# Splitting the query and key fetches of a hybrid decoder trunk, with full-height score products and new planner costs

## The chip, the cores and the metric

The kernel runs on one core of one Trainium2 chip. The metric is the device time of one execution in microseconds (us); several executions are timed and their median is given. TensorE (PE) multiplies, VectorE (DVE), ScalarE (ACT) and GpSimd (POOL) work elementwise, and DMA transfers are issued from the queues of SyncE (SP), POOL and ACT.

## The reference

The reference is a decoder trunk of two layers on 512 tokens of 1024 channels. Each layer is FFN, token mixer, FFN, each followed by a layer norm. The mixer has three head groups that read one projection and feed one output projection:

```python
x = layer_norm(ALPHA * x + 0.5 * swiglu(x, gate_a, up_a, down_a))
aq, ak, av, bq, bk, bv, cc = split(x @ w_in)
o_a = diff_attention(rope(aq), rope(ak), av, lam)    # 6 heads, two softmax maps each, q and k 32 wide
o_b = dilated_attention(rope(bq), rope(bk), bv)      # 6 heads, q and k 64 wide, three dilation patterns
o_c = rwkv7_mixer(cc, ...)                           # 4 heads, recurrent state 64 x 64 per head
x = layer_norm(ALPHA * x + concat(o_a, o_b, o_c) @ w_out)
x = layer_norm(ALPHA * x + 0.5 * swiglu(x, gate_b, up_b, down_b))
```

## The kernel before, in words

All big products are float32 made of three products of rounded parts: a value is split into a high part (rounded to the fast float32r form) and a low part (the rest), and hi x hi, hi x lo and lo x hi are added up (`mm3`). The FFNs are written as plain loops. They take most of the time and the change leaves them alone.

The mixer of each layer is different. It is written as some 24 Python generators (`columns` for the input projection, `turner`, `fetch`, `attend` for both attention groups, `keys`, `inside`, `invert`, `scan`, `rwkv_out` for the recurrent group, `out` for the output projection, and more). `Board.merge` runs them against a table of estimated costs and estimated free times. It always takes the first generator in a fixed rank that is ready by these estimates, and so fixes the order in which every engine gets its instructions. On the chip each engine then works strictly in that written order, and waits where an operand is not there yet. An estimate that is wrong therefore costs nothing by itself; it only changes the order.

Queries and keys of the two attention groups go a detour. `turner` transposes them on PE, splits them into a high and a low part in a tile `z`, and SP stores them to memory (`qkA`, `qkB`, three head pairs each). `fetch`, on POOL's queue, loads them back, one head (`e` is 0 or 1 in the pair `hp`) at a time, in the arrangement that the score product needs. A fetch waits for the pair's stores and for two free slots of the tag `x` (four in all). On POOL the fetches stand in one line with the computation of the low parts of the weights (`wl`) and with the masks of the recurrent group (`x<-am`).

For group A the contraction is 96 rows high: rows 0 to 31 hold hi, 32 to 63 lo, 64 to 95 hi of the query, against hi, hi and lo of the key. Before, two transfers per tile fill this, and the first has a source whose outermost dimension counts 2 (stride `256 * S` between the high and low parts for the query, stride 0 for the key, so that it is read twice):

```python
dma(a[0:64], ap(d, hi, [[256 * S, 2], [2 * S, 32], [1, 2 * S]]))
dma(b[0:64], ap(d, hi + k, [[0, 2], [2 * S, 32], [1, 2 * S]]))
```

For group B the query's hi and lo stand above each other in 128 rows and meet the key's hi in both halves; a second product of 64 rows adds the query's hi times the key's lo (`b`, 64 rows).

Each POOL transfer signals on one of eight semaphores, taken in turn; a transfer waits until the one eight places before it has landed.

`scan` walks the recurrent group's eight chunks of 64 tokens: each needs the state of the one before, and `sgm` is that state times the decay. `rwkv_out` normalizes each pair of chunks (tiles `gy`, `yc`), and `mixer_tiles_c` transposes `yc` on PE (`m<-kept,yc`) for the output projection. The second half of the scan loads its tiles `kr` back from memory through SP's queue.

Of the kernel before, what the change touches and what calls it, by code (L numbers as in the profile page):

```python
# [369 lines left out]
class Board:  # L370
# [36 lines left out]
    def note(self, name, fn, aps, cost):  # L407
        at = self.free[name]
        tiles = [self.ready.setdefault(a.tensor.name, [0.0, "", 0.0, None]) for a in aps]
        assert all(r[3] != "dropped" for r in tiles)  # L410
        dma = fn == "dma_start"
        for r in tiles[dma and tiles[0][1] == "dma":]:
            if r[1] != name or name != "pe":
                at = max(at, r[0] + 0.134)
        end = at + cost
        self.free[name] = end
        if dma:
            n = 4
            for d in aps[0].shape:
                n *= d  # L420
            end = max(end, self.free["dma"]) + n / 340e3
            self.free["dma"] = end
            end += 2.0
        for r in tiles:
            r[2] = max(r[2], end)
        tiles[0][0] = max(tiles[0][0], end)
        tiles[0][1] = "dma" if dma else name
        if dma:
            self.late = max(self.late, end)
        elif name != "pe":  # L430
            self.last = max(self.last, end)
# [45 lines left out]
class Watched:  # L477
# [5 lines left out]
    def __getattr__(self, fn):  # L483
        call = getattr(self.engine, fn)

        def run(*args, **kw):
            aps = [a for a in list(args) + list(kw.values()) if hasattr(a, "tensor") and hasattr(a, "shape")]
            n = 1
            for a in aps:
                m = 1  # L490
                for d in a.shape[1:]:
                    m *= d
                n = max(n, m)
            if self.name == "pe":
                n = 1
                for d in aps[0].shape[1:]:
                    n *= d
                rate = 2 if fn == "transpose" else 1 if aps[2].dtype == FR and n >= 256 else 4
                cost = rate * n / 2400.0 + (0.009 if rate == 4 else 0.003)
            elif fn == "dma_start":  # L500
                cost = {"pool": 1.04, "act": 0.5, "sp": 0.47}[self.name]
            elif fn == "reciprocal":
                cost = 0.06 + n / 160.0
            else:
                cost = {"vec": 0.07 + n / 960.0, "act": 0.12 + n / 1400.0, "pool": 0.1 + n / 720.0}[self.name]
                if fn == "activation" and "accum_out" in kw:
                    cost += 0.1
                if fn == "tensor_tensor" and self.name == "pool":
                    cost = 0.1 + n / 450.0
            self.board.note(self.name, fn, aps, cost)  # L510
            return call(*args, **kw)  # L511

        return run
# [7 lines left out]
class Mix:  # L521
# [247 lines left out]
    def fetch(self):  # L769

        dma = self.gps.dma_start
        ap = lambda t, off, dims: bass.AP(tensor=t.tensor, offset=t.offset + off, ap=dims)
        for grp in "AB":
            for hp in range(3):
                for e in range(2):
                    yield f"qk{grp}{hp}", "x", "x"
                    if (hp, e) == (0, 0):
                        yield f"qk{grp}{hp}", "x", "x", "bias"
                        self.bias = self.get("bias", "bias")
                        dma(self.bias, self.tr.consts[:, 130:642] if grp == "A" else self.tr.consts[:, 642:1154])  # L780
                    a = self.get("x", "q", (128, 2, S))
                    d = self.qk[grp, hp]
                    hi, lo, k = e * 64 * S, (256 + e * 64) * S, 128 * S
                    if grp == "A":
                        b = self.get("x", "k", (128, 2, S))
                        dma(a[0:64], ap(d, hi, [[256 * S, 2], [2 * S, 32], [1, 2 * S]]))
                        dma(b[0:64], ap(d, hi + k, [[0, 2], [2 * S, 32], [1, 2 * S]]))
                        dma(a[64:96], ap(d, hi, [[2 * S, 32], [1, 2 * S]]))
                        dma(b[64:96], ap(d, lo + k, [[2 * S, 32], [1, 2 * S]]))
                    else:  # L790
                        b = self.get("x", "k2", (64, S))
                        dma(a[:, 0, :], ap(d, hi, [[256 * S, 2], [S, 64], [1, S]]))
                        dma(a[:, 1, :], ap(d, hi + k, [[0, 2], [S, 64], [1, S]]))
                        dma(b, ap(d, lo + k, [[S, 64], [1, S]]))
                    self.qkt[grp, hp, e] = a.bitcast(FR), b.bitcast(FR)
                    self.mark(f"q{grp}{hp}{e}")

# [308 lines left out]
    def scan(self):  # L1106

        vec, act, pe, sp = self.vec, self.act, self.pe, self.sp
        u, drop, kr, am, bt, yt, gam = self.u, self.drop, self.kr, self.am, self.bt, self.yt, self.gam
        st = None  # L1110
        yield "yt0"
        for ch in range(8):
            hf, cc = divmod(ch, 4)
            if cc == 0:
                yield "u", "u"
                for j in range(2):
                    kr[j, hf] = u("kr", (128, 4, 2, 64))
                    sp.dma_start(kr[j, hf].rearrange("p c e t -> p (c e t)"), self.kd[j, hf])
                yield f"yt{hf}", kr[0, hf], kr[1, hf]
            yield f"uv{ch // 2}"  # L1120
            uv, vt = self.uv[ch // 2]
            uvc = uv[:, ch % 2]
            heads = [(h, h // 2, HALF[h % 2], HALF[1 - h % 2], am[hf, h % 2, cc // 2][:, cc % 2, h // 2]) for h in range(4)]
            yield ".", "r"
            z = self.acc("r", (128, 2, 64))
            for h, j, s, f, a_ in heads:
                pe.matmul(z[f, j, :], a_[s, 0:64], uvc[s, h, :], start=True, stop=st is None)
                if st is not None:
                    pe.matmul(z[f, j, :], kr[j, hf][s, cc, 0, :], st[s, j, :], start=False, stop=True)
            zs = self.t("zs", (128, 2, 64), bufs=2)  # L1130
            act.copy(zs, z)
            drop(z)
            yield ".", "r"
            ups = self.acc("r", (128, 2, 64))
            for h, j, s, f, a_ in heads:
                pe.matmul(ups[f, j, :], yt[hf][f, cc * 2 + j, :], zs[f, j, :], start=True, stop=True)
            act.mul(uvc[HALF[1], 0::2], ups[HALF[1]], -1.0)
            vec.tensor_scalar(uvc[HALF[0], 1::2], ups[HALF[0]], -1.0, None, op0=OP.mult)
            drop(ups)
            nst = None  # L1140
            if ch < 7:
                yield ".", "r", "st"
                ps = self.acc("r", (128, 2, 64))
                for h, j, s, f, a_ in heads:
                    pe.matmul(ps[s, j, :], bt[hf, cc // 2][:, cc % 2, j, s], uvc[:, h, :], start=True, stop=True)
                nst = self.get("st", "st", (128, 2, 64))
                for j in range(2):
                    gj = gam[j][:, ch:ch + 1]
                    if st is None:
                        vec.tensor_scalar(nst[:, j, :], ps[:, j, :], gj, None, op0=OP.mult)  # L1150
                    else:
                        vec.scalar_tensor_tensor(nst[:, j, :], ps[:, j, :], gj, sgm[:, j, :], op0=OP.mult, op1=OP.add)
                drop(ps)
                if ch < 6:
                    sgm = self.t("sgm", (128, 2, 64), bufs=2)
                    for j in range(2):
                        vec.tensor_scalar(sgm[:, j, :], nst[:, j, :], gam[j][:, ch + 1:ch + 2], None, op0=OP.mult)
            if cc == 3:
                drop(yt[hf], bt[hf, 0], bt[hf, 1])
            self.chunks.append((ch, uv, st, heads, kr, vt, am))  # L1160
            self.mark(f"chunk{ch}")
            st = nst
# [62 lines left out]
    def attend(self, grp):  # L1225
# [6 lines left out]
        def scores(x):  # L1232
# [7 lines left out]
            for m in range(M):  # L1240
                sc = self.acc("p1")
                if isA:
                    pe.matmul(sc[:, :nn], a[0:96, m, qs], b[0:96, m, :nn], start=True, stop=True)
                else:
                    pe.matmul(sc[:, :nn], a[:, 0, qs], a[:, 1, :nn], start=True, stop=False)
                    pe.matmul(sc[:, :nn], a[0:64, 0, qs], b[:, :nn], start=False, stop=True)
                t = self.get("t", "t")
                nm = self.t("nm", (128, 1), bufs=8)
                vec.tensor_tensor_reduce(t[:, :n], sc[:, :n], bias[:, S - n:], scale, 3e38, op0=OP.add, op1=OP.min,
# [300 lines left out]
```

## Time and profile before

| what | value |
|---|---|
| median of 3 runs | 2329.84 us (2324.28 to 2331.13) |
| the profiled execution's own time | 2319.83 us |
| its span, first to last instruction | 2318.0 us |
| PE busy | 2215.6 us (96% of the span) |
| mean granted clock of PE | 0.975 |
| DVE, ACT, POOL busy | 49%, 35%, 14% |
| mixer of layer 0 and of layer 1 | about 376 to 800 us and 1523 to 1957 us |

The profiled execution is 10.0 us faster than the median of the timed runs. Times in rows are microseconds from the start of the span. A busy PE is a PE with a product in its pipeline, which says nothing of the clock that it has: a granted clock of 1.00 is 2.4 GHz, 0.50 is 1.2 GHz.

### The profile page before, as it was taken

Reading aid. Unit: us, or ns where it says so; the run is one execution under the profiler, and the core shown is the slowest. Engines: PE = TensorE matmul, PEld = TensorE weight load, DVE = VectorE, ACT = ScalarE, POOL = GpSimd, SP = SyncE. Lnnn points to the kernel's source line nnn. Section 1 sums busy time; section 2 is a strip of 40 time slices with the busy share of each in tenths; the row PEclk is TensorE's granted clock in tenths of the full one; section 3 lists DMA queues with packets and bytes.
Section 4 is the critical chain, followed back from the end, with each engine's and each line's share of the span. In section 5 each row is a group of like instructions: output and inputs, shape, how many; then the busy total and the mean of one; then the engine's idle time right before and its main releaser. Section 6 shows DMA issues by size and latency. Waiting matters only on the chain.

```text
span 2318.0 us, 31736 instructions
## 1 busy us (share of the span) xinstructions
PE 2215.6 (96%) x12384; PEld 1863.6 (80%) x12384; DVE 1146.8 (49%) x2483; ACT 803.4 (35%) x1559; POOL 317.5 (14%) x344
## 2 busy tenths in 40 slices
PE   9999999988899999999999999999878999999998
PEld 8888888787776788888888888887877867888886
DVE  3333346766566633333653332656765666333336
ACT  4322223435444323222433222343444443222222
POOL 1000002343232200000010000033432322000000
PEclk9999999999899999999999999999987999999999
DMA  5333344354433323332543333432553323233334
GB/s 171 101 102 98 113 137 146 102 136 98 104 106 101 118 74 94 98 99 91 173 120 108 101 96 109 155 128 85 136 108 94 107 95 119 84 98 91 100 109 154
DMA packets 253030, 258.34 MB, mean 111 GB/s; under 512 B 45562, under 2 KB 202304, under 8 KB 252880
## 3 DMA queue, kind: packets, MB, share of 16 engines
q1 hardware_dynamic: 221488, 228.20, 32.4%
q0 software_dynamic: 30816, 27.06, 4.8%
q8 instruction: 97, 1.59, 0.3%
q10 hardware_dynamic: 576, 1.05, 0.1%
q14 instruction: 53, 0.43, 0.1%
HBM read 233.85 MB, written 22.28 MB: 110 GB/s over the span
## 4 chain that ended last, share of the span: by engine, by line
PE 80%; DVE 8%; DMA 5%; issue 4%; POOL 1%; ACT 1%; SPq 0%; POOLq 0%; DVEq 0%; ACTq 0%
PE p L87 18%; PE p L86 18%; PE p L85 18%; PE p L511 13%; PE m L511 4%; PE r L511 3%; DMA k<-qkA 3%; PE r L86 2%; PE r L85 2%; PE r L87 2%; DMA k<-qkB 1%; DVE x L511 1%; POOL wl L511 1%; DMA q<-qkB 0%; DVE x L146 0%
## 5 line engine op out<-in xcount | busy, mean ns | idle before, releaser
L80 DVE TENSOR_TENSOR lo<-raw,hi 128x1024 fp32r<-128x1024 f32 x300 | 366.2, 1223 | 627.8 <-ACT hi L79 627.5
L87 PE MATMUL p<-xhi,lo 128*128 128x512 f32 (+1 forms) x1392 | 535.7, 385 | 0.0
L86 PE MATMUL p<-xlo,hi 128*128 128x512 f32 (+1 forms) x1392 | 533.7, 383 | 0.7 <-DVE xlo L126 0.7
L85 PE MATMUL p<-xhi,hi 128*128 128x512 f32 (+1 forms) x1392 | 533.6, 383 | 0.5 <-ACT xhi L125 0.5
L79 ACT CAST hi<-raw 128x1024 fp32r<-128x1024 f32 x300 | 315.6, 1053 | 583.5 <-PE p L86 258.1
L86 PEld LDWEIGHTS p<-xlo,hi 128*128 128x128 f32 x1392 | 261.7, 188 | 56.3 <-DVE xlo L126 1.1
L85 PEld LDWEIGHTS p<-xhi,hi 128*128 128x128 f32 x1392 | 261.8, 188 | 53.8 <-ACT xhi L125 1.0
L87 PEld LDWEIGHTS p<-xhi,lo 128*128 128x128 f32 x1392 | 261.9, 188 | 52.6
L511 POOL TENSOR_TENSOR wl<-wr,wh 128x512 fp32r<-128x512 f32 x152 | 203.8, 1360 | 670.1 <-ACT wh L511 629.3
L511 PE MATMUL p<-wh,xhi 128*128 128x256 f32 (+1 forms) x704 | 233.7, 332 | 1.4 <-DVE rb L511 1.1
L511 PE MATMUL p<-wh,xlo 128*128 128x256 f32 (+1 forms) x704 | 218.9, 311 | 0.5 <-DVE xlo L511 0.4
L511 PE MATMUL p<-wl,xhi 128*128 128x256 f32 (+1 forms) x704 | 218.5, 310 | 0.0
L87 PE MATMUL p<-hi,hl 128*128 128x512 f32 x528 | 205.8, 390 | 0.0
L86 PE MATMUL p<-lo,hh 128*128 128x512 f32 x528 | 205.8, 390 | 0.0
L85 PE MATMUL p<-hi,hh 128*128 128x512 f32 x528 | 205.7, 390 | 0.0
L511 PEld LDWEIGHTS p<-wh,xhi 128*128 128x128 f32 x704 | 138.9, 197 | 12.7 <-PE p L511 1.5
L511 PEld LDWEIGHTS p<-wh,xlo 128*128 128x128 f32 x704 | 138.7, 197 | 7.6 <-DVE xlo L511 2.2
L246 DVE TENSOR_TENSOR hr<-p,hr 128x512 f32<-128x512 f32 x88 | 60.8, 691 | 167.3 <-PE p L87 156.9
L511 PEld LDWEIGHTS p<-wl,xhi 128*128 128x128 f32 x704 | 139.2, 198 | 4.3
L247 ACT CAST hh<-hr 128x512 fp32r<-128x512 f32 x88 | 54.3, 617 | 205.9 <-DVE hr L246 195.8
L511 ACT ACTIVATE t<-t,nm 128x128 f32<-128x128 f32 (+3 forms) x144 | 80.2, 557 | 125.0 <-DVE nm L511 124.0
L85 PEld LDWEIGHTS p<-hi,hh 128*128 128x128 f32 x528 | 99.1, 188 | 20.6
(253 smaller groups left out, 3061.0 us busy)
## 6 DMA issues: line engine op xcount, KB each, us to landing
raw<-in_ffn_a_down SPq DMA_DIRECT2D x66, 512.0 KB, 3.3
raw<-in_ffn_b_down SPq DMA_DIRECT2D x66, 512.0 KB, 3.3
raw<-in_ffn_a_gate SPq DMA_DIRECT2D x44, 512.0 KB, 3.8
raw<-in_ffn_a_up SPq DMA_DIRECT2D x44, 512.0 KB, 3.9
raw<-in_ffn_b_gate SPq DMA_DIRECT2D x40, 512.0 KB, 3.9
raw<-in_ffn_b_up SPq DMA_DIRECT2D x40, 512.0 KB, 3.8
wr<-in_w_in SPq DMA_DIRECT2D x56, 256.0 KB, 3.1
wr<-in_w_in SPq DMA_DIRECT2D x24, 512.0 KB, 3.8
```

Of the source, the lines that this page charges most:

```text
L79: nc.scalar.copy(hi, raw)
L80: (vec or nc.vector).tensor_tensor(lo, raw, hi.bitcast(FT), op=OP.subtract)
L85: mm(out, lh, rh, start=first, stop=False)
L86: mm(out, lh, rl, start=False, stop=False)
L87: mm(out, ll, rh, start=False, stop=last)
L246: nc.vector.tensor_tensor(hr, acc[1, f], hr, op=OP.mult)
L247: nc.scalar.copy(hi, hr)
L511: return call(*args, **kw)
```

## The change

The fetches of group A become six transfers of 32 rows per head instead of four, those of group B six of 64 rows instead of three; no source has an outermost dimension of 2 any more. Group B's low key stands in both halves of a tile of 128 rows, so that the second score product has 128 rows too (it adds lo x lo, which was left out before). The decayed state `sgm` is computed by ACT instead of DVE. And the planner's costs of PE products, POOL transfers and the transfer rate are changed, which orders the mixer of both layers anew.

```diff
-            end = max(end, self.free["dma"]) + n / 340e3
+            end = max(end, self.free["dma"]) + n / 300e3
...
-                rate = 2 if fn == "transpose" else 1 if aps[2].dtype == FR and n >= 256 else 4
-                cost = rate * n / 2400.0 + (0.009 if rate == 4 else 0.003)
+                if fn != "transpose" and aps[2].dtype == FR and n >= 256:
+                    cost = n / 2286.0 + 0.0055
+                else:
+                    m = 1
+                    for d in aps[1].shape[1:]:
+                        m *= d
+                    cost = max(n, m) / 1200.0 + 0.004
             elif fn == "dma_start":
-                cost = {"pool": 1.04, "act": 0.5, "sp": 0.47}[self.name]
+                cost = {"pool": 0.65, "act": 0.5, "sp": 0.47}[self.name]
...
-                        dma(a[0:64], ap(d, hi, [[256 * S, 2], [2 * S, 32], [1, 2 * S]]))
-                        dma(b[0:64], ap(d, hi + k, [[0, 2], [2 * S, 32], [1, 2 * S]]))
-                        dma(a[64:96], ap(d, hi, [[2 * S, 32], [1, 2 * S]]))
-                        dma(b[64:96], ap(d, lo + k, [[2 * S, 32], [1, 2 * S]]))
+                        for n, (q, r) in enumerate(((hi, hi), (lo, hi), (hi, lo))):
+                            rows = slice(32 * n, 32 * n + 32)
+                            dma(a[rows], ap(d, q, [[2 * S, 32], [1, 2 * S]]))
+                            dma(b[rows], ap(d, r + k, [[2 * S, 32], [1, 2 * S]]))
                     else:
-                        b = self.get("x", "k2", (64, S))
-                        dma(a[:, 0, :], ap(d, hi, [[256 * S, 2], [S, 64], [1, S]]))
-                        dma(a[:, 1, :], ap(d, hi + k, [[0, 2], [S, 64], [1, S]]))
-                        dma(b, ap(d, lo + k, [[S, 64], [1, S]]))
+                        b = self.get("x", "k2", (128, S))
+                        for rows, q in zip(HALF, (hi, lo)):
+                            dma(a[rows, 0, :], ap(d, q, [[S, 64], [1, S]]))
+                            dma(a[rows, 1, :], ap(d, hi + k, [[S, 64], [1, S]]))
+                            dma(b[rows], ap(d, lo + k, [[S, 64], [1, S]]))
...
-                        vec.tensor_scalar(sgm[:, j, :], nst[:, j, :], gam[j][:, ch + 1:ch + 2], None, op0=OP.mult)
+                        act.activation(sgm[:, j, :], nst[:, j, :], AF.Copy, scale=gam[j][:, ch + 1:ch + 2])
...
-                    pe.matmul(sc[:, :nn], a[0:64, 0, qs], b[:, :nn], start=False, stop=True)
+                    pe.matmul(sc[:, :nn], a[:, 0, qs], b[:, :nn], start=False, stop=True)
```

The first place is POOL's line at the first fetch of layer 0, pair 0 of group A, both heads. Before:

```order
L511 DMA q_3939<-qkA0_0_2684 64x1x1024
L511 DMA k_3940<-qkA0_0_2684 64x1x1024
L511 DMA q_3939<-qkA0_0_2684 32x1024
L511 DMA k_3940<-qkA0_0_2684 32x1024
L511 DMA q_3945<-qkA0_0_2684 64x1x1024
L511 DMA k_3946<-qkA0_0_2684 64x1x1024
L511 DMA q_3945<-qkA0_0_2684 32x1024
L511 DMA k_3946<-qkA0_0_2684 32x1024
L511 TENSOR_TENSOR wl_3988<-wr_3851,wh_3987 128x512
```

In the changed program the same place has twelve transfers (the weights' low parts follow behind them, as before):

```order
L516 DMA q_3912<-qkA0_0_2684 32x1024
L516 DMA k_3913<-qkA0_0_2684 32x1024
L516 DMA q_3912<-qkA0_0_2684 32x1024
L516 DMA k_3913<-qkA0_0_2684 32x1024
L516 DMA q_3912<-qkA0_0_2684 32x1024
L516 DMA k_3913<-qkA0_0_2684 32x1024
L516 DMA q_3920<-qkA0_0_2684 32x1024
L516 DMA k_3921<-qkA0_0_2684 32x1024
L516 DMA q_3920<-qkA0_0_2684 32x1024
L516 DMA k_3921<-qkA0_0_2684 32x1024
L516 DMA q_3920<-qkA0_0_2684 32x1024
L516 DMA k_3921<-qkA0_0_2684 32x1024
```

The low parts `wl` move behind four more transfers, and the ninth transfer is the first that shares a semaphore with one of its own batch.

The second place is SP's line in layer 0 where group B's queries and keys are stored and the second half of the scan gets its `kr`. Before:

```order
L511 DMA wr<-in_w_in 128x4x128 x2
L511 DMA kr<-kr_2690 128x512 x2
L511 DMA wr<-in_w_out 128x2x512 x2
L511 DMA qkB_1_2688<-z 128x4x128 x3
L511 DMA wr<-in_w_out 128x2x512
```

And in the changed program:

```order
L516 DMA wr<-in_w_out 128x2x512
L516 DMA qkB_1_2688<-z 128x4x128
L516 DMA kr<-kr_2690 128x512 x2
L516 DMA qkB_2_2689<-z 128x4x128 x2
L516 DMA wr<-in_w_out 128x2x512 x2
```

The load of `kr` moves behind all four stores of pair 1 of group B and behind four loads of the output weights, so the second half of the scan starts later in the mixer.

The third place is PE's line in layer 0 between the last products of the recurrent group (`m<-st,kr`) and the transposes of the last `yc`. In the changed program six products of the output projection stand between the last chunk and the transposes of the third `yc`, and twelve more ahead of those of the fourth:

```order
L516 MATMUL m<-uv,am 64x64
L516 MATMUL m<-st,kr 64x64
L516 MATMUL p_7226<-wh,xhi 128x512
L516 MATMUL p_7226<-wl,xhi 128x512
L516 MATMUL p_7226<-wh,xlo 128x512
L516 MATMUL p_7227<-wh,xhi 128x512
L516 MATMUL p_7227<-wl,xhi 128x512
L516 MATMUL p_7227<-wh,xlo 128x512
L516 MATMUL m<-kept,yc 128x128 x2
```

Before, a run of 57 such products ended at the transposes of the fourth `yc`; its last ones are these:

```order
L511 MATMUL p_7273<-wh,xhi 128x512
L511 MATMUL p_7273<-wl,xhi 128x512
L511 MATMUL p_7273<-wh,xlo 128x512
L511 MATMUL p_7274<-wh,xhi 128x512
L511 MATMUL p_7274<-wl,xhi 128x512
L511 MATMUL p_7274<-wh,xlo 128x512
L511 MATMUL m<-kept,yc 128x128 x2
```

So 18 products instead of 57 lie between the last chunk and the last `yc` in layer 0; in layer 1 there are 33.

## Rows read from the trace of the kernel before

**Rows 1.** The page, busy time and chain that ended last.
```profile
PE 2215.6 (96%) x12384; PEld 1863.6 (80%) x12384; DVE 1146.8 (49%) x2483; ACT 803.4 (35%) x1559; POOL 317.5 (14%) x344
...
PE p L87 18%; PE p L86 18%; PE p L85 18%; PE p L511 13%; PE m L511 4%; PE r L511 3%; DMA k<-qkA 3%; PE r L86 2%; PE r L85 2%; PE r L87 2%; DMA k<-qkB 1%; DVE x L511 1%; POOL wl L511 1%; DMA q<-qkB 0%; DVE x L146 0%
```

**Rows 2.** Waits of PE: total us, times, longest.
```profile
PE p L511 <- DMA k<-qkA: 38.7, 6, 11.5
PE m L511 <- DVE xlo L511: 10.9, 8, 1.9
```

**Rows 3.** Windows, mixer of layer 0: busy us of each engine, PE clock, DMA share.
```profile
376.00:800.00 424.00, 380.42 (x2867) 329.16 (x2866) 280.21 (x866) 178.55 (x518) 144.03 (x147) 0.94 0.39 108
```

**Rows 4.** Timeline of PE: three of the six waits for group A's keys.
```profile
506.02 0.76 PE L511 MATMUL p<-k,q 96*128 96x256 f32 x2 [3.50 <-DMA k<-qkA]
...
1700.71 0.77 PE L511 MATMUL p<-k,q 96*128 96x256 f32 x2 [11.54 <-DMA k<-qkA]
1743.82 0.77 PE L511 MATMUL p<-k,q 96*128 96x256 f32 x2 [4.97 <-DMA k<-qkA]
```

**Rows 5.** The chain in time: start, and us from issue to landing.
```profile
1681.02 19.45 DMA k<-qkA
```

**Rows 6.** Timeline of POOL: two first issues of fetches.
```profile
492.56 0.69 POOL L511 DMA_DIRECT2D q<-qkA  x1 [1.57 <-issue]
...
1731.45 0.70 POOL L511 DMA_DIRECT2D q<-qkA  x1 [1.05 <-DMA qkA<-z]
```

**Rows 7.** DMA issues on POOL's queue: count, KB each, median us to landing.
```profile
x<-x POOLq DMA_DIRECT2D x8, 512.0 KB, 4.3
q<-qkA POOLq DMA_DIRECT2D x12, 256.0 KB, 12.4
...
k<-qkA POOLq DMA_DIRECT2D x12, 128.0 KB, 12.1
...
bias<-in_constants POOLq DMA_DIRECT2D x4, 256.0 KB, 3.5
gb<-in_ln_b POOLq DMA_DIRECT2D x2, 512.0 KB, 7.1
```

**Rows 8.** Windows right behind the six waits: first of six, and their sum.
```profile
506.00:509.10 3.10, 3.08 (x14) 3.10 (x15) 1.30 (x9) 1.20 (x5) 0.00 (x0) 0.50 0.44 90
...
sum 35.80, PE 35.67 PEld 34.71 DVE 21.10 ACT 15.19 POOL 1.81; mean PE 5.94 PEld 5.78 DVE 3.52 ACT 2.53 POOL 0.30
```

**Rows 9.** Timeline of PE: a score of group B, and products of the FFN.
```profile
717.90 0.48 PE L511 MATMUL p<-q 128*128 128x512 f32 x1
718.31 0.50 PE L511 MATMUL p<-k,q 64*128 64x512 f32 x1
718.74 0.33 PE L511 MATMUL m<-kept,t 128*128 128x128 f32 x1
...
860.63 0.40 PE L87 MATMUL p<-xhi,lo 128*128 128x512 f32 x1
860.86 0.40 PE L85 MATMUL p<-xhi,hi 128*128 128x512 f32 x1
```

**Rows 10.** Timeline of ACT and PE: steps of one chunk of the scan.
```profile
682.52 0.27 ACT L511 COPY zs<-r 128x128 f32<-128x128 f32 x1 [0.90 <-PE r L511]
684.95 0.45 PE L511 MATMUL r<-uv,bt 128*64 128x64 f32 x8
```

**Rows 11.** Timeline of DVE: norm of the last chunks of layer 0.
```profile
744.53 0.23 DVE L511 BATCH_NORM_STATS2 gst<-gy 128x6 f32<-128x64 f32 x1 [3.12 <-ACT gy L511]
...
752.70 0.41 DVE L511 TENSOR_TENSOR gy<-gy,gg 128x256 f32<-128x256 f32 x1
```

**Rows 12.** Groups by line and form on POOL: count, busy us, mean ns, idle before.
```profile
L511 POOL TENSOR_TENSOR wl<-wr,wh 128x512 fp32r<-128x512 f32 x152 | 203.8, 1360 | 670.1 <-ACT wh L511 629.3 <-PE p L511 27.2 <-PE r L511 13.0
L511 POOL DMA_DIRECT2D q<-qkB x24 | 19.6, 825 | 23.4 <-PE m L511 15.0 <-DMA qkB<-z 7.3 <-issue 0.8
L511 POOL DMA_DIRECT2D k<-qkB x12 | 7.0, 583 | 0.0
```

## The prediction

> **What bounds the kernel now.** The page comes first: PE is busy for 2215.6 of 2318.0 us, and the chain that ended last is PE work for the greatest part, with one strange guest, the landing of group A's keys, at 3% [rows 1]. The FFNs are solid PE work and the change doesn't touch them, so the question is what PE does in the two mixers. The windows show 380.4 busy us in 424 for layer 0, and a mean clock of 0.94 [rows 3]: some 44 us idle, and some time at half clock. The waits of PE say whose idle time that is. Six waits for `k<-qkA` make 38.7 us over both layers; the next group makes 10.9 us in eight pieces of at most 1.9 [rows 2]. Behind each of the six waits PE runs at 1.2 GHz for a while: the six stretches last 35.8 us, PE is busy in 35.67 of them, and the first shows a clock of 0.50 [rows 8]. So fetches that land late cost twice, once in idle time and once in clock.
>
> Why are they late? A fetch of 256 KB takes a median of 12.4 us from issue to landing. On the same queue the bias, also 256 KB, takes 3.5 us, and the residual, 512 KB, takes 4.3 [rows 7]. The size doesn't explain it. What sets the fetches apart is the source: outermost dimension 2, where the others have 128 rows.
>
> **The change part by part.**
>
> *The fetches of group A.* How early must the data be there? PE came to the first score at 506.02 - 3.50 = 502.5, which is 10.0 us after the first issue at 492.56. The tightest of the six is the last: 1743.82 - 4.97 = 1738.9, 7.4 us after 1731.45 [rows 4, 6]. Now six transfers per head, at some 0.58 us an issue (the 64-row transfer of group B, the nearest row that is not of the wide form [rows 12]): the last of them is issued 2.9 us after the first. If it then lands as the residual does, in 4.3 us, the head is there after 7.2 us; if as the slow `gb`, 7.1 us, after 10.0 [rows 7]. The first is in time for all six, the second misses the tightest by 2.6 us. The six waits thus shrink from 38.7 to between 0 and about 3; I take 2.5 left over, a gain of 36. If the split doesn't make a transfer faster, the bound on the other side is no gain at all.
>
> The trace shows the slow landing [rows 7], not its reason. The Trainium skill, "DMA: Bandwidth & Descriptors", section "Rules for kernel authors", has one: an outermost dimension of c < 16 confines a DMA to at most c of the 16 DMA engines. By that page's 27 GiB/s an engine, 128 KB on each of two engines would take about 4.5 us (an estimate from the page), against 0.6 on sixteen; each of the six waits would then shrink by about 4 us at most, which gives some 23 us in place of 36.
>
> *The clock.* With the waits the stretches at half clock behind them should go. At most that gives back half of 35.8 us, 17.9 [rows 8]; at least nothing, since short waits can keep the clock down too. PE is busy in practically all of them, so I take 14.
>
> *The second score product of group B.* A 512-column product of full height starts 0.23 us before the next in the FFN (860.63, 860.86). Between the 128-row `p<-q` and the 64-row `p<-k,q` it is 0.41, and from there to the next 128-row instruction 0.43 [rows 9]: each change of height costs about 0.19 us. With 128 rows both changes vanish: 0.38 us for each of 24 scores in each of two layers, 18.2 us if narrower scores pay as much. As a lower bound nothing, if PE then waits for DVE or ACT instead. PE waits little in the mixer [rows 2], so I take 15.
>
> *The new order.* It moves two things against PE. First, the norm of the last chunk in layer 0. From its first DVE instruction at 744.53 to the product with the gate at 752.70 + 0.41 it takes 8.6 us [rows 11], and after the change only 18 products of 0.23 us, 4.2 us, cover it on PE: 4.4 us late. In layer 1 it is 33 products, 7.7 us: 0.9 late. Second, the scan's second half comes later, because its `kr` is loaded later on SP, and its last chunks have only the output projection to hide behind. From the `zs` copy at 682.52 to the third product group at 684.95 two hand-offs take 2.4 us [rows 10], and three output products, 0.7 us, stand in most gaps: about 1.2 us open per chunk, two late chunks in each layer, 5 us. Together a loss of 10. It could be 0, since an order can also close gaps, or 25, if half of the 16 chunks lie open for 2.4 us and the norms stay late.
>
> The new costs themselves are mixed. A 512-column fast product is now put at 0.230 us, and the trace has 0.23. A 64-column float32 product is put at 0.057 or 0.111 where it was 0.116, and four of them, eight instructions, take 0.45 us, so 0.11 [rows 9, 10]. The planner now often believes PE to be further on than it is, which puts more work between dependent steps: a reason for late scans, and against many new waits.
>
> *At nothing.* POOL issues more: for group B 2 x 0.825 + 0.583 = 2.2 us per head become 6 x 0.583 = 3.5, 12 heads, 15 us; for group A some 10. It is hidden because POOL waits 629 us for ACT between the `wl` [rows 12]; uncovered it would be 25 us. `sgm`, 24 small instructions, moves from DVE to ACT. At the 0.27 us of the `zs` copy [rows 10], the nearest row on ACT, that is 6.5 us more there, and ACT is busy for 178.6 of 424 us [rows 3]; the next chunk needs it three product groups later. Uncovered, 6.5 us. The extra 128 KB per head of group B, 1.5 MB, rides on a DMA share of 0.39 [rows 3].
>
> *The sum.* 36 + 14 + 15 - 10 = 55 us. The profiled execution took 2319.83 us, so 2265 us for one like it. The median of the runs is 10.0 us above that, and the difference carries over: 2329.84 - 55 = 2275 us.
>
> **The rivals.**
>
> *Half of it stays.* The twelve transfers of a batch use eight semaphores. If a transfer lands later than 8 x 0.58 = 4.6 us, the ninth is held, and the `wl` queue up behind it on POOL; PE and SP's weight loads wait for those. For it speaks one key that took 19.45 us to land amid other traffic [rows 5]; against it that 3.5 and 4.3 us are the medians of plain loads on this queue [rows 7]. With half the waits and half the clock left: 18 + 7 + 15 - 10 = 30, so 2300 us.
>
> *The split changes nothing.* All transfers share the same engines and the traffic of SP, and the fetch is late because its bytes are. For it speaks that the 32-row transfers of 128 KB, issued behind the wide ones, land no sooner (12.1 us); against it that they stand in one queue with these, and the bias and the residual [rows 7]. Then 15 - 10 = 5: 2325 us. The Trainium skill, the same page and section, advises against splits of this kind: two transfers to disjoint partition halves serialize, and one of 128 partitions is to be preferred. By that rule, this case would come; the rows bear it out only for shapes that already spread.
>
> *The order ruins it.* The recurrent chain becomes what PE waits for. If all 16 chunks show their two hand-offs in full, 16 x 2.4 = 39 us, and all eight norms are late by 4.4 us, 35 us, the loss is 74 instead of 10, against gains of 65: 2329.84 + 9 = 2339 us. It decides from 65 us of open hand-offs on. Against it: before, PE's other waits are short [rows 2], and there are some 40 us of output products at the mixer's end to hide behind.
>
> **How the numbers follow.** The forecast has a chance of 0.70, half of it 0.17, no effect of the split 0.07, the ruined order 0.06. A difference below 0.3%, 7 us, can't be told from none. Faster by more are the first two, 0.87; within it the third, 0.07; slower the fourth, 0.06. The likeliest case alone spans 2246 (all gains in full, 36 + 2.5 + 17.9 + 18.2 = 75, and an order that closes another 9 us) to 2292. The range reaches on to the half case with some room, 2246 to 2310, and leaves out the last two.
>
> **What would show it.** Right: landings of `q<-qkA` and `k<-qkA` of 3 to 6 us; no wait of PE for them above 3 us; full clock where the six stretches were; 0.23 us from `p<-q` to `p<-k,q` at 512 columns; a wait of some 4 us ahead of the last `m<-kept,yc` in layer 0. Wrong: landings still near 12 us; POOL idle inside a batch of twelve; new waits of PE for `wl`, `zs` or `uv` of more than 20 us in all. The prediction fails if the reordered mixers, not the fetches, decide.

## The result and the profile after

| | before | after |
|---|---|---|
| median | 2330.49 us (4 runs) | 2294.78 us (4 runs, 2292.59 to 2299.22) |
| ratio | | 0.9844, 95% interval 0.9807 to 0.9881 |
| span of the profiled execution | 2318.0 us | 2292.4 us |

The kernel became 1.6% faster, 36 us by the medians; 55 were forecast (2275 us). The time lies inside the range, outside the 2246 to 2292 given for the likeliest case. The profiled execution of after lies at its median, that of before some 10 us below it, so the two traces differ by 25.6 us only. All comparisons of stages below are between traces, one execution of each kernel.

The chain that ended last in the changed kernel; the landing of group A's keys has left the chain [rows 1]:

```profile
PE p L87 19%; PE p L86 18%; PE p L85 18%; PE p L516 15%; PE r L516 5%; PE m L516 4%; PE r L86 2%; PE r L85 2%; PE r L87 2%; DVE x L516 1%; DVE t L516 1%; DVE bk L516 0%; DVE x L146 0%; DVE l L516 0%; DVE xlo L516 0%
```

Its DMA issues on POOL's queue (count, KB each, median us to landing), to set against [rows 7]: the fetches land in 4.7 and 4.9 us instead of 12.

```profile
q<-qkA POOLq DMA_DIRECT2D x36, 128.0 KB, 4.7
k<-qkA POOLq DMA_DIRECT2D x36, 128.0 KB, 4.9
```

Its waits of PE (total us, times, longest), to set against [rows 2]. The 38.7 us are down to 2.2, and one wait of 3.2 us ahead of the first score of group A in layer 1 ("issue": the profile shows nothing that it waited for). But the list has new heads: `rs_y`, `o`, `yc`, `gb`, and more for `xlo`.

```profile
PE m L516 <- DVE xlo L516: 17.1, 9, 3.9
PE r L516 <- DVE rs_y L516: 9.4, 4, 3.1
PE m L516 <- DVE o L516: 6.4, 3, 3.2
...
PE m L516 <- DVE yc L516: 4.9, 3, 3.2
PE p L516 <- issue: 3.2, 1, 3.2
PE m L516 <- DVE gb L516: 3.2, 4, 1.1
...
PE p L516 <- DMA k<-qkA: 2.2, 2, 2.0
...
PE r L516 <- ACT zs L516: 1.5, 3, 0.6
```

The windows of the two mixers, first before, then after (us, busy us of each engine, PE's clock, DMA share, GB/s). Each window holds the same number of PE products in both kernels, but for one, so that its ends stand at the same work. The part of a mixer in which PE is not busy is idle time. How long PE is busy for the same products depends on their size and on the clock.

```profile
379.00:813.10 434.10, 390.51 (x2964) 339.79 (x2963) 283.51 (x869) 183.82 (x523) 141.12 (x145) 0.94 0.39 111
1525.90:1968.90 443.00, 397.79 (x2973) 344.53 (x2972) 285.67 (x875) 188.75 (x528) 139.91 (x142) 0.93 0.39 108
```

```profile
378.40:799.40 421.00, 385.70 (x2964) 336.24 (x2963) 276.50 (x857) 186.41 (x535) 148.81 (x175) 0.95 0.40 116
1512.10:1939.00 426.90, 392.80 (x2972) 338.92 (x2971) 280.41 (x863) 191.07 (x540) 148.15 (x172) 0.94 0.39 114
```

The two mixers together became 29.2 us shorter (877.1 to 847.9): 19.4 us of idle time (88.8 to 69.4) and 9.8 of busy time. Some 33 us of waiting for keys are gone (38.7 to 2.2 and 3.2), yet idle time fell by 19 only, and the clock hardly rose. Something gave half of it back.

### The profile page after: what moved, and what is told of

The parts are those of the page before. It is cut to its first block, busy times and chain, and to the rows that moved or that the text cites. A ratio compares the mean times of both kernels' runs of the same rounds, so it can differ in the third digit from the quotient of the medians.

```text
span 2292.4 us, 31827 instructions
## 1 busy us (share of the span) xinstructions
PE 2209.4 (96%) x12384; PEld 1856.4 (81%) x12384; DVE 1134.4 (49%) x2459; ACT 808.1 (35%) x1583; POOL 333.5 (15%) x404
## 4 chain that ended last, share of the span: by engine, by line
PE 85%; DVE 9%; ACT 2%; issue 2%; DMA 1%; POOL 1%; SPq 0%; DVEq 0%; ACTq 0%; POOLq 0%
PE p L87 19%; PE p L86 18%; PE p L85 18%; PE p L516 15%; PE r L516 5%; PE m L516 4%; PE r L86 2%; PE r L85 2%; PE r L87 2%; DVE x L516 1%; DVE t L516 1%; DVE bk L516 0%; DVE x L146 0%; DVE l L516 0%; DVE xlo L516 0%
## 5 line engine op out<-in xcount | busy, mean ns | idle before, releaser
L87 PEld LDWEIGHTS p<-hi,hl 128*128 128x128 f32 x528 | 99.2, 188 | 20.6
```

What stands on the lines that cost most here:

```text
L87: mm(out, ll, rh, start=False, stop=last)
```

## The experiments

Two things were changed at once: what is executed (fetches, rows, `sgm`) and the order. They can be taken apart, since the planner only hears of costs. A kernel may tell it of the old transfers and issue others; then PE, DVE, ACT and SP keep the old order row for row. The traces show it: in e1, e2, e3, e5 and e6 all 12,384 products of PE stand in the order of before; in the last three of these, ACT has the 24 instructions for `sgm` instead of DVE. The table has all runs, each ratio against runs of the kernel before on the same chip (e1 to e4, e5 to e8, e9 to e11 and e12 ran on four chips); the last three columns come from windows of the two mixers as above.

| kernel | median us | ratio (95%) | mixers us | PE busy | idle |
|---|---|---|---|---|---|
| before | 2330.49 | 1 | 877.1 | 788.3 | 88.8 |
| after | 2294.78 | 0.9844 (0.9807 to 0.9881) | 847.9 | 778.5 | 69.4 |
| e1_split | 2258.77 | 0.9698 (0.9662 to 0.9735) | 813.6 | 768.9 | 44.7 |
| e2_rows | 2318.56 | 0.9957 (0.9933 to 0.9980) | 872.8 | 776.6 | 96.2 |
| e3_all_old_order | 2246.63 | 0.9655 (0.9617 to 0.9694) | 805.1 | 753.3 | 51.9 |
| e4_new_order | 2394.97 | 1.0270 (1.0227 to 1.0314) | 955.4 | 846.4 | 109.0 |
| e5_interleave | 2256.16 | 0.9701 (0.9645 to 0.9756) | 812.9 | 759.6 | 53.3 |
| e6_small2 | 2291.02 | 0.9866 (0.9796 to 0.9937) | 840.8 | 769.7 | 71.1 |
| e7_old_pe_costs | 2298.84 | 0.9883 (0.9821 to 0.9945) | 854.5 | 783.9 | 70.6 |
| e8_old_dma_costs | 2293.77 | 0.9862 (0.9805 to 0.9918) | 848.4 | 781.9 | 66.5 |
| e9_fill | 2283.54 | 0.9819 (0.9795 to 0.9843) | 839.0 | 786.4 | 52.6 |
| e10_old_order_fill | 2252.86 | 0.9677 (0.9650 to 0.9705) | 811.7 | 773.7 | 38.1 |
| e11_old_pool108 | 2307.37 | 0.9918 (0.9891 to 0.9944) | 858.1 | 791.8 | 66.3 |
| e12_fill_nox | 2275.93 | 0.9754 (0.9728 to 0.9780) | 832.6 | 777.4 | 55.2 |

**What is executed, and the order (e1 to e4).** In e1, and likewise in e2 and e3, the fetch tells the planner of the old transfers and issues its own:

```diff
-                        dma(a[0:64], ap(d, hi, [[256 * S, 2], [2 * S, 32], [1, 2 * S]]))
...
+                    note = lambda t: self.board.note("pool", "dma_start", [t, d], 1.04)
...
+                        for t in (a[0:64], b[0:64], a[64:96], b[64:96]):
+                            note(t)
...
+                    raw = self.nc.gpsimd.dma_start
...
+                            raw(a[rows], ap(d, q, [[2 * S, 32], [1, 2 * S]]))
...
```

> Order of every engine as before; only the fetches are split as in the change (second score product still 64 rows, decay on VectorE). Theory 1 (the fetch is worth what the forecast said, 36 us of wait and 14 of clock, and the new order takes some 20 back): 2330 - 50 = 2280 us, total wait of PE for k<-qkA under 3 us, the half-clock stretches behind the six waits gone. Theory 2 (the waits go, but their time comes back as other waits and the low clock stays wherever PE works on small products): 2330 - 20 = 2310 us, half-clock time of the mixers still about 100 us. Theory 3 (the split does nothing, the order brings the gain): 2330 us.

> Order of every engine as before, fetches with the wide outermost-2 form as before, one more 64-row transfer per head of group B that fills the lower half of the low key, second score product of group B with 128 rows (lo x lo is added). Theory 1: 15 us faster, 2315 us, waits for k<-qkA still near 39 us. Theory 2: PE then waits for VectorE and ScalarE in place of the height changes: under 5 us faster, 2326 us. Theory 3 as theory 1.

> Split fetches, 128-row products and decay on ScalarE as in the change, but every engine in the order of before. What the new order costs is the changed kernel less this one. Theory 1: 2330 - 50 - 15 = 2265 us, so the new order costs 30 us. Theory 2: 2330 - 20 - 12 = 2298 us, so the new order costs nothing. Theory 3: 2315 us, the new order gains 20 us.

e4 is the reverse: the planner of the changed kernel hears of the new transfers, the old ones are issued.

> The order of the changed kernel on every engine, but the old fetches with outermost dimension 2, 64-row second products and decay on VectorE. Theory 1: the new order costs 30 us also with the old fetch, 2360 us, or less where the new waits hide behind the late fetch: 2335 to 2360 us. Theory 2: 2330 us. Theory 3: 2310 us.

By the ratios the split alone is worth 70 us (interval 62 to 79), where theory 1 had 50; the 128 rows 10 (5 to 16), where it had 15; all edits together 80 (71 to 89), where it had 65. The new order costs 44 us on top of them (0.9844 against 0.9655, give or take 12), where it had 30, and 63 on top of the old fetch: e4 takes 2395 us, above the 2335 to 2360 of theory 1. So theory 1 has the signs right and every size but that of the rows too small; the other two fall, though the waits that theory 2 named for the rows do come (e2, below). `sgm` has nothing left to explain within these intervals (70 + 10 against 80); it was not run alone. In e1's waits of PE `k<-qkA` doesn't occur; among the first are these:

```profile
PE m L511 <- DVE xlo L511: 10.9, 8, 1.9
...
PE r L511 <- DVE rs_y L511: 4.3, 2, 2.1
```

The windows of the mixers, e1 and then e3:

```profile
382.10:788.20 406.10, 383.07 (x2965) 332.69 (x2963) 277.81 (x869) 183.75 (x523) 146.05 (x169) 0.97 0.40 118
1497.00:1904.50 407.50, 385.84 (x2972) 333.55 (x2972) 280.63 (x875) 187.57 (x528) 145.92 (x166) 0.97 0.39 117
```

```profile
380.40:784.30 403.90, 378.61 (x2964) 333.46 (x2963) 275.94 (x857) 185.72 (x535) 149.58 (x175) 0.96 0.41 121
1493.20:1894.40 401.20, 374.64 (x2972) 328.09 (x2971) 280.34 (x863) 189.96 (x540) 148.84 (x172) 0.99 0.41 121
```

PE has the same products in the same order before and in e1, and is busy for 19.4 us less. That is the clock: its mean rises from 0.94 and 0.93 to 0.97 in both mixers, and by the clock records of the traces the half-clock stretches of the mixers shrink from 109 us to 48. Idle time falls by 44.1. After against e3, the same products in two orders: 25.2 us more busy, 17.6 us more idle, and 99 us of half clock against 41. The order is paid mostly in clock.

e2's waits of PE show why 128 rows bring less than the products save. PE is busy for 11.7 us less than before, and waits 5.5 us more for `xlo` and 6.2 more for `q<-qkB`, for which it had waited 1.7 us before:

```profile
PE p L511 <- DMA k<-qkA: 36.9, 6, 11.0
PE m L511 <- DVE xlo L511: 16.4, 8, 3.9
PE p L511 <- DMA q<-qkB: 7.9, 4, 3.0
```

**Which property of the fetch (e5, e6).** Both are e3 with another fetch. The edit of e5 exchanges two dimensions and splits nothing. That of e6 splits into six, and keeps the 2 outermost in four of group A's six transfers and in all of group B's. For group A's query:

```diff
-   [[256 * S, 2], [2 * S, 32], [1, 2 * S]]      # before
+   [[2 * S, 32], [256 * S, 2], [1, 2 * S]]      # e5
+   [[256 * S, 2], [2 * S, 16], [1, 2 * S]]      # e6, twice
```

> As e3_all_old_order, but the fetches are not split: the wide transfers of the kernel before (256 KB and 128 KB, four per head of group A, three per head of group B) with their two outer dimensions exchanged, so that the source counts 32 or 64 at its outermost and 2 inside, for the same bytes. The contraction's rows then alternate high and low parts, the sums are the same. If the outermost count of 2 made the landing slow: landings of 3 to 5 us, waits for k<-qkA under 3 us, 2247 us as e3_all_old_order or some us less. If what helped was the splitting into six smaller transfers: landings still near 12 us and 2315 us, as e2_rows.

> As e3_all_old_order, with six transfers per head of the same sizes as in the change, but four of group A's and all but none of group B's six have a source that counts 2 at its outermost (high and low part of 16 or 32 rows). If the outermost count is the cause: landings of 8 to 12 us, waits for k<-qkA of 25 us or more, about 2300 us. If the size of a transfer is the cause: landings of 4 us and 2247 us.

DMA issues of e5, then of e6:

```profile
q<-qkB POOLq DMA_DIRECT2D x24, 256.0 KB, 4.0
...
q<-qkA POOLq DMA_DIRECT2D x12, 256.0 KB, 5.2
k<-qkA POOLq DMA_DIRECT2D x12, 256.0 KB, 5.7
```

```profile
q<-qkB POOLq DMA_DIRECT2D x48, 128.0 KB, 7.6
q<-qkA POOLq DMA_DIRECT2D x36, 128.0 KB, 7.4
k<-qkA POOLq DMA_DIRECT2D x36, 128.0 KB, 7.5
```

The outermost count of 2 is the cause: exchanged, the wide transfers land in 4.0 to 5.8 us without any splitting, PE waits for no `k<-qkA`, and the time is that of e3 within the intervals. With small transfers that keep the 2 it takes 7.4 to 7.7 us, PE waits for fetches again (`q<-qkB` 12.8 us, `k<-qkA` 6.8, `q<-qkA` 4.2), and the median is 44 us above e3's. This is less than was expected of e6 (landings of 8 to 12 us, 25 us for `k<-qkA`): smaller transfers take part of the delay away even with the 2 kept. The rule of the Trainium skill that the prediction weighed, "DMA: Bandwidth & Descriptors", "Rules for kernel authors" (an outermost dimension of c < 16 confines a DMA to at most c engines), agrees in direction. By its 27 GiB/s an engine, 128 KB on two engines would take some 2.0 us longer than on sixteen (an estimate from the page); e6 against e3, which lands group A's fetches in 4.8 and 5.1 us, shows 2.4 to 2.6. How many engines a transfer used no row here shows. The trace also agrees with the other rule of the same section, that splitting by partitions gains nothing: e5 without it does as well as e3 with it, within the intervals. The case that the prediction drew from it (2325 us) did not come, because this split also took the 2 away.

**Which of the new costs (e7, e8, e11).** e7 keeps the old formula for products, e8 the old transfer costs and list, both with all else as in the change. e11 is e3 with the planner told 1.08 us in place of 1.04 for a transfer on POOL.

> The changed kernel with the old cost formula for PE's products in the planner; transfers and their new costs as in the change. The order is a third one. If the new product costs (small float32 products now believed to be twice as cheap) make the order worse: near 2250 us, idle gaps of PE in the two mixers near 52 us, low clock near 41 us. If the new transfer costs do: near 2295 us.

> The changed kernel with the old transfer costs in the planner (old list of transfers, 1.04 us an issue, 340 GB/s), and the new costs of PE's products. If the new product costs make the order worse: near 2295 us, gaps near 69 us, low clock near 99 us. If the new transfer costs do: near 2250 us. Both near 2270 us if each brings half.

> As e3_all_old_order, but the planner is told 1.08 us in place of 1.04 us for each of the old list of transfers on POOL, all other costs as before: a different order out of the old costs. If the new costs as such make orders worse: near 2250 us. If the order of before is merely one of few good ones, which any change of costs loses: 2280 to 2300 us, with gaps and low clock like those of the changed kernel.

Read by themselves, e7 blames the transfer costs and e8 the product costs: undoing either half leaves the time where it was, so either half alone loses the good order. e11 shows the rest. One old cost moved by 4% gives an order that is 61 us slower than e3 (0.9918 against 0.9655), with 66 us of idle time, as in the changed kernel; at 2307 us it is even above the 2280 to 2300 expected. With the new fetches, four orders lie between 2294 and 2307 us and one at 2247: it is the order of before that is good, and every re-planning that was tried loses it. How rare such an order is, five can't tell. Why the others share some 66 to 71 us of idle time was not settled.

**Does the clock follow the waits (e9, e10, e12)?** Behind the wait of 3.25 us for `o`, late in layer 1 of the changed kernel, the clock stays at half (timeline of PE: start, us, idle before):

```profile
1844.27 1.11 PE L516 MATMUL m<-kept,o 128*128 128x128 f32 x4 [3.25 <-DVE o L516]
...
1848.15 0.48 PE L516 MATMUL m<-uv,am 128*64 128x64 f32 x2
1848.56 0.47 PE L516 MATMUL m<-st,kr 64*64 64x64 f32 x2
```

Windows of such stretches of the changed kernel, behind the waits for `rs_y`, the first key, `yc` and `o`:

```profile
440.60:447.40 6.80, 6.80 (x15) 3.78 (x14) 2.29 (x5) 1.83 (x3) 0.00 (x0) 0.50 0.25 73
508.90:512.30 3.40, 3.40 (x18) 3.30 (x17) 1.74 (x8) 1.67 (x7) 0.39 (x1) 0.50 0.93 128
747.80:751.20 3.40, 3.40 (x9) 2.60 (x8) 1.07 (x3) 1.24 (x2) 1.55 (x2) 0.50 0.00 0
1843.50:1860.50 17.00, 15.37 (x56) 10.73 (x57) 8.10 (x35) 3.24 (x8) 0.00 (x0) 0.50 0.11 32
```

It could be the wait, or the small products of the recurrent group that stand there. So the waits are filled with products of no use (here ahead of the transposes of `o`):

```diff
             tp = self.acc("m", (128, 4, 128))
+            self.fill(tp[:, 0, :], "o", n)
             for t in range(NT):
                 self.pe.transpose(tp[:, t, :], o[:, t], tr.ident)
```

> The changed kernel with idle PE time filled: ahead of the instructions on which PE waits longest (transposes of rs_y, x, o and yc, and the first score of group A, both layers) stand 2 to 14 extra float32 products of 128 columns with the identity, whose result the following transposes or products overwrite. No operand is waited for earlier or later, the order of all else is that of the change. If the low clock follows the waits: the half-clock stretches behind these places go, some 81 of 99 us, worth up to 40 us, 2255 to 2275 us. If the low clock comes from the small products of the recurrent group in the new order themselves: the stretches stay where they are and the time is 2295 us or some us more.

> As e3_all_old_order, with the same kind of filling at the waits that are left in that order (rs_y, x, yc, and three of the rope tiles). If the low clock follows the waits: of its 41 us of half clock most go, worth 10 to 20 us: 2227 to 2237 us. If not: 2247 us or some us more.

> As e9_fill without the 50 extra products ahead of the transposes of x (8, 3 and 14 in each layer). In e9_fill these waited themselves (for the bank that the xlo before them still read: 3.92 us, as without them), so they filled nothing and stood in the way, and the low clock behind them stayed. If the price of the low clock is half of its time: 50 products of some 0.22 us less, 2283 - 11 = 2272 us, with the low clock of the mixers still near 41 us. If low clock is cheap, and filling brings nothing but the extra products' time: 2283 us or 2290 us.

In e12 the same place has twelve extra products (two instructions each, 24 in the row shown), a wait of 0.58 us, and behind it the same small products at full clock, 0.26 us a pair in place of 0.41 (timeline, then a window from there on):

```profile
1829.17 2.84 PE L578 MATMUL m<-kept 128*128 128x128 f32 x24
1832.59 0.66 PE L517 MATMUL m<-kept,o 128*128 128x128 f32 x4 [0.58 <-DVE o L517]
...
1836.12 0.33 PE L517 MATMUL m<-uv,am 128*64 128x64 f32 x2
1836.38 0.33 PE L517 MATMUL m<-st,kr 64*64 64x64 f32 x2
```

```profile
1837.00:1852.00 15.00, 13.54 (x70) 9.39 (x71) 10.98 (x42) 2.72 (x7) 1.29 (x1) 1.00 0.00 0
```

e9 holds its own control. Ahead of the transposes of `x` its products waited for `xlo` themselves (for the bank from which it was still being made), so that the wait remained, and so did half clock around it:

```profile
1895.49 0.80 PE L578 MATMUL m<-kept 128*128 128x128 f32 x2 [3.92 <-DVE xlo L517]
```

So at the filled places the low clock followed the wait, and not the kind of product. Half clock in the mixers falls from 99 us to 41 in e9 and 48 in e12 (clock records). e9 nevertheless takes 2284 us, 6 us better than the changed kernel by the ratios, and misses its 2255 to 2275. Without those 50 useless products e12 takes 2276 us where 2272 were expected, 0.9754 against 0.9844 of the changed kernel: some 21 us, give or take 11, for nothing but keeping PE busy.

The wait is not the whole story. In layer 0 of the changed kernel the clock falls in the middle of an unbroken run of small products, with no wait since one of 0.83 us at 713.48: the pair that took 0.26 us takes 0.41 from 717.07 on. e12, which fills nothing there, shows the same at 712.69. What part the small products have in this was not separated.

```profile
713.48 0.33 PE L516 MATMUL m<-uv,am 128*64 128x64 f32 x2 [0.83 <-DVE gb L516]
...
716.82 0.33 PE L516 MATMUL m<-st,kr 64*64 64x64 f32 x2
717.07 0.48 PE L516 MATMUL m<-uv,am 128*64 128x64 f32 x2
717.48 0.47 PE L516 MATMUL m<-st,kr 64*64 64x64 f32 x2
```

In the old order (e10) the same filling gains nothing, 2253 us against 2247, where 2227 to 2237 were expected. Idle time fell by 14 us and half clock only from 41 us to 31, while the 110 extra products (0.24 us each by the row of e12) raised the busy time by 20.

e3 is the fastest of all versions: by the ratios 3.5% below the kernel before and 1.9% below the changed one.

## Why the prediction was right, and where it was off

*The fetches of group A.* Right, and slightly too small: landing below 5 us, and no wait for them above 3.2 us (3 was the limit set). 36 us were forecast; idle time falls by 44.1 in e1, group B's fetches included.

*The clock.* Forecast 14, bounded by 17.9. In the old order the split gives 19.4, beyond the bound, which looked only at the stretches right behind the six waits. In the changed kernel nothing of it is left: its busy time is 9.8 us less, and the 128 rows alone save 11.7 (e2). The sign "full clock where the six stretches were" holds for e1; in the changed kernel 3.4 us at half clock stand behind the first key (window above).

*The second product.* The mechanism is there, if not in full: 0.31 us from `p<-q` to `p<-k,q`, where 0.23 was forecast, and 0.23 to the next, where it was 0.41 and 0.43 before [rows 9]. That is 0.30 us less for a score instead of 0.38.

```profile
688.00 0.48 PE L516 MATMUL p<-q 128*128 128x512 f32 x1
688.31 0.39 PE L516 MATMUL p<-k,q 128*128 128x512 f32 x1
688.54 0.27 PE L516 MATMUL m<-kept,t 128*128 128x128 f32 x1
```

The size is 10 instead of 15: PE is busy for 11.7 us less in e2, and then waits for DVE and for `q<-qkB`.

*The new order.* This is the step that failed: "Together a loss of 10." It measured 44, beyond the 25 named as its upper end. The two places that it went by behaved: the last `yc` of layer 0 comes 3.19 us late (4.4 forecast, line below), and the hand-offs of the scan show as 1.5 us (`zs`) where 5 were forecast. The loss sits at other places. Against e3 (lines below) PE waits 5.1 us more for `rs_y`, 2.8 for `xlo`, 2.5 for `gb`, 6.4 for `o`, which is no wait at all in e3, and 4.3 for the first fetches; some waits of e3 are gone in turn (`rc`), and net idle time is 17.6 us more. And the loss has a second part that the forecast charged to the old waits only: the lower clock, 25.2 us.

```profile
746.61 0.41 PE L516 MATMUL m<-kept,yc 128*128 128x128 f32 x2 [3.19 <-DVE yc L516]
```

e3's waits of PE:

```profile
PE m L511 <- DVE xlo L511: 14.3, 8, 3.9
...
PE r L511 <- DVE rs_y L511: 4.3, 2, 2.1
```

*At nothing.* `sgm` and the extra transfers of group B stayed hidden: e3, with both, is 12 us faster than e1 by the medians, about what the rows bring by themselves. The extra issues of group A are in e1 already, where PE waits for a fetch for 0.6 us in all.

*The rivals.* "Half of it stays" gives 2300 us, closest to the result, for a wrong reason: the waits for keys did go, and the longest that the landing of an earlier fetch held up another is 1.61 us (the twelfth of its batch, first line below). A longer hold, 2.77 us ahead of the fourth transfer in layer 1, waits for nothing that the profile shows, and the 3.2 us of PE at the first score there follow it; its cause stays open. "The split changes nothing" is refuted by e1. "The order ruins it" names the right place, but the price was 44 us, below the 65 at which it decides.

```profile
575.49 0.49 POOL L516 DMA_DIRECT2D k<-qkA  x1 [1.61 <-DMA k<-qkA]
...
1642.95 0.49 POOL L516 DMA_DIRECT2D k<-qkA  x1 [2.77 <-issue]
```

In all: gains of 80 instead of 65, a loss of 44 instead of 10, net 36 instead of 55. The mechanism of the gain was right; that the time lies in the range at all is partly luck, since the gains were put too low by 15 us and the loss by 34, and the two errors offset in part.

## What to carry to other kernels

In this kernel a source whose outermost dimension is 2 made transfers on POOL's queue land late (medians of 9 to 13 us instead of 3.5 to 6); exchanging the dimensions cured it as well as splitting did. A change that also re-plans an order should be measured with the old order held fixed: here the plan cost more than half of what the edits gained. And a wait of PE that an order adds is to be priced twice, as idle time and as the half clock that can follow it.

## What the runs showed of the hardware that was not expected

The outer-2 form also multiplies packets on POOL's DMA queue. These are the page's lines on all packets and on that queue (packets, MB, share), before and then in e1, for nearly the same bytes. All of the 20,736 packets that e1 has less are under 512 B, and both traces have 6,528 packets of 4,096 B on that queue: the data itself was not cut smaller. Every run with the 2 outermost has these packets and the late landings, so the runs don't separate the two.

```profile
DMA packets 253030, 258.34 MB, mean 111 GB/s; under 512 B 45562, under 2 KB 202304, under 8 KB 252880
...
q0 software_dynamic: 30816, 27.06, 4.8%
```

```profile
DMA packets 232294, 258.21 MB, mean 115 GB/s; under 512 B 24826, under 2 KB 181568, under 8 KB 232144
...
q0 software_dynamic: 10080, 26.94, 4.3%
```

Behind single waits of 2 to 3.3 us PE ran at half clock for 3.4 to 17 us of its work (windows above), and once behind a wait of 0.83 us amid small products.

The FFN behind the last mixer took 344.6 us in the trace of after and 340.4 in that of before, with 1491 products and a clock of 1.00 in both. This offsets 4.2 of the 29.2 us that the mixers gained; its cause stays open.
